# A second block product of the scan's gate in front of the attention scores, with buffers re-homed and the later order re-planned

## Chip, cores and metric

The kernel runs on one core of a Trainium2 chip. The metric is the device time of one execution in microseconds (us). "Before" is the kernel as it was, "after" the kernel with the change.

## What is computed

One decoder layer on 256 tokens of width 1024, batch 1, all in float32. Both branches, a gated linear recurrence (the "scan", HGRN2) and a softmax attention that here has one block of 256 keys, start from one normalised input and one wide projection:

```
h = rmsnorm(x, attn_norm_g)
hq, hf, hi, hg, aq, ak, av, gl = split(h @ w_in)
y_hg = (rmsnorm(scan(hq, hf, hi)) * silu(hg)) @ w_branch_hg
att  = softmax(rmsnorm(aq) . rmsnorm(ak) * scale + bias, causal) @ av
y_at = att @ w_branch_attn
merged = sigmoid(gl[0]) * y_hg + sigmoid(gl[1]) * y_at
x = x + merged @ w_out
x = x + (silu(n @ w_ffn_gate) * (n @ w_ffn_up)) @ w_ffn_down     with n = rmsnorm(x, ffn_norm_g)
```

There are 8 heads of width 128 in either branch.

## The kernel before

**Precision and halves.** Every float32 factor of a large product is split into a high half and a low half, both in the format fp32r. A weight block of 128 x 2048 numbers is loaded (`L:`), its high half is cast on ScalarE (ACT; step `h:`, line 500) and its low half, the difference, is made on VectorE (DVE; step `l:`, line 504). The matrix engine TensorE (PE) then makes the product (`M:`): for a block of 512 x 512 weights, eight 128x512 matmuls with the high half and then four with the low half (`product`, line 523). Three buffers each hold raw, high and low blocks in turn, so a new `h:` or `L:` also waits for the use of the third one before it.

**Seven products for eight.** The gates (`GS`, the silu gate of the scan; `GY` and `GZ`, the two sigmoid gates) are projected by a scheme with seven block products in place of eight. Products 1 and 2 take the weight blocks as they are (w11, w21). The others take sums that are made in place: block 5 is w11 + w12, block 6 adds w22 to that, block 7 is w12 + w22, block 4 is w21 plus the sum of block 6. Such a sum is either an addition on VectorE (`S:`, line 594) or a DMA that adds while it copies, issued from GpSimd's queue (`A:`, line 600); the tuple `BY_DMA` says which. So the sum of block 6 may be written only when both halves of block 5 are taken from the same buffer: `h:GS5`, `l:GS5`, `A:GS6`, `h:GS6`, `l:GS6`, `M:GS6` is a chain.

**The order.** The first part of the program, up to the attention scores, is ordered by the framework's scheduler by priority. From there on the order is written out by hand as two lists of names, `MIDDLE` and `FFN`; each name is one step, and each engine gets its steps in the order of the list. Every engine works strictly in its own order and waits where a step's input or a buffer is not ready. The stage of interest in `MIDDLE` has these steps:

- `scores` (PE line 482, DVE line 486): queries times keys; VectorE scales them and adds the bias, into `S0` (first 128 queries) and `S1` (last 128).
- `xa`, `xb0`, `xb1` (DVE 815): row maxima; `ea`, `eb0`, `eb1` (ACT 819): exponentials with their sums; `ma`, `mb0`, `mb1` (DVE 822, 823): division by the sums. `a` is `S0`, `b0` and `b1` are the two halves of the heads of `S1`.
- `M:p0` to `M:p5` (PE 839): transposes of the probabilities, through three PSUM banks in turn; `M:p0` and `M:p2` need `mb0`, `M:p1` and `M:p3` need `mb1`, the other two `ma`. `i:` copies each out on ScalarE (846, 851) and `k:` makes the low half on VectorE (853).
- `M:v` (PE 875, 878): probabilities times values, with the values' halves `vh` (ACT 863) and `vl` (DVE 866).
- `M:V2`, `M:V3` (PE 658): the projection of half of the values; `c:V0`, `c:V1` copy it out (ACT 905).
- `E3` to `E6`: levels of the scan (`k` ACT 379, `M` PE 394, `b` DVE 401, `q` DVE 416, `d` DVE 424).
- `Ch0`, `Ch1` (ACT 558) and `Cl0`, `Cl1` (DVE 561): halves of sums of the input that products 3, 5, 6 and 7 read.

In the kernel before only `GS1` stands in front of the scores; `GS2` stands in `MIDDLE`, between the transposes of the probabilities, because its weight block w21 is loaded into the buffer of the keys (home `T9`), which the scores read last.

**Homes.** Large buffers share named homes (`T1`, `T2`, ...): a buffer with the same tag may be written only when the last reader of the one before it is done.

Of the kernel before, what the change touches and what calls it, by code (L numbers as in the profile page):

```python
# [7 lines left out]
F32 = mybir.dt.float32  # L8
F32R = mybir.dt.float32r
# [18 lines left out]
def tile_hgrn2_moba_block(ctx: ExitStack, tc: tile.TileContext, xm, xw, table, runs,  # L28
# [3 lines left out]
    big = ctx.enter_context(tc.tile_pool(name="big", bufs=1))  # L32
# [123 lines left out]
    V0 = [pw(), pw()]  # L156
    V1 = [pw(), pw()]
# [10 lines left out]
    for kt in range(KT):  # L168
        i = kt % 2
# [4 lines left out]
        xk = packed[kt][:, 0:S] if kt else packed[kt][:, NV:NX]  # L174
# [30 lines left out]
    for q in range(2):  # L205
# [62 lines left out]
    R = big.tile([P, S], F32, name="R", tag="R")  # L268
# [74 lines left out]
    A = big.tile([P, 2, H, P], F32, name="A", tag="T5")  # L343
# [126 lines left out]
    def scores(qtok, qss, kT):  # L470
        rq = small.tile([P, 2, H], F32, name="rq")
        rinv(rq, qss, P)
        qT = head_T(qtok, "T10", "qT", qg[:, 0:1])
        S0 = big.tile([P, H, P], F32, name="S0", tag="T13")
        S1 = big.tile([P, H, S], F32, name="S1", tag="T7")
        for sc, tb, w, bt in ((S0, 0, P, B0), (S1, 1, S, B1)):
            m = 512 // w
            for g in range(H // m):
                bank = (pa, ph)[g % 2]()
                for i in range(m):  # L480
                    h = m * g + i
                    nc.tensor.matmul(bank[:, i * w:(i + 1) * w], qT[:, h, tb * P:(tb + 1) * P], kT[:, h, 0:w],
                                     start=True, stop=True)
                for i in range(m):
                    h = m * g + i
                    nc.vector.scalar_tensor_tensor(sc[:, h, :], bank[:, i * w:(i + 1) * w], rq[:, tb, h:h + 1],
                                                   bt[:, h, :], op0=OP.mult, op1=OP.add)
# [95 lines left out]
    def scheme(u, x, sums, bank_of, put):  # L583
# [14 lines left out]
        for k, a, other in (("5", "11", "12"), ("6", "11", "22"), ("7", "12", "22"), ("4", "21", "11")):  # L598
            if u.name + k in BY_DMA:
                todo[f"A:{u.name}{k}"] = lambda a=a, other=other: nc.gpsimd.dma_start(u.w[a], u.w[other], accum_op=OP.add)  # L600
# [21 lines left out]
            todo[("x:" if u.gate else "s:") + u.name + k] = lambda k=k, i=i, j=j: \  # L622
                put(i, j, banks[0] if k == "4" else q(i, j), j if k != "4" else 0)

    BY_DMA = ("GA4", "GA7", "GB4", "GB5", "GB7", "GS4", "GS5", "GS6", "GS7", "GY7", "GZ4", "GZ7", "UA4", "UA5", "UA7", "UB4", "UB7")

    four = []

# [13 lines left out]
    M = []  # L642
# [57 lines left out]
    hgrn_level(2)  # L700
    Va = big.tile([P, 2, D], F32, name="Va", tag="T1")
    put_tok(Va, tok_block(w_in, 6144, XT), 0)
    for name in ("L:V2", "L:V3", "L:GSw11", "h:GS1", "l:GS1", "M:GS1"):
        todo.pop(name)()
    S0, S1 = scores(qtok, qss, kT)
    hgrn_level(3, pa)

# [67 lines left out]
    oT = []  # L775
# [7 lines left out]

    def turned_o(g, m):
        if g % 2 == 0 and m == 0:
            oT.append(big.tile([P, 4, 2, S], F32R, name=f"oT{g // 2}", tag=("T6", "T9")[g // 2]))
        src = bank4(3).rearrange("p (h t) -> p h t", h=2)
        dst = [oT[g // 2][:, 2 * g % 4:2 * g % 4 + 2, k, :] for k in range(2)]
        if m == 0:
            nc.scalar.mul(dst[0], src, og)  # L790
        else:
            nc.vector.scalar_tensor_tensor(dst[1], src, og, dst[0].bitcast(F32), op0=OP.mult, op1=OP.subtract)
# [3 lines left out]
        todo[f"i:To{g}"] = lambda g=g: turned_o(g, 0)  # L796
        todo[f"k:To{g}"] = lambda g=g: turned_o(g, 1)

    GY = Unit("GY", w_in, 8192, ("T12", "T13"), ("T9", "T5", "T1", "T4"))
    GZ = Unit("GZ", w_in, 7168, "T4", ("T8", "T5", "T1", "T7"))  # L800

    for u in (GY, GZ):
        scheme(u, XT, sums, bank4, gate_of(u, AF.Sigmoid))
# [37 lines left out]
    def turned_p(n, m):  # L841
        hs, cs = slice(4 * (n % 2), 4 * (n % 2) + 4), turns_of[n][2]
        if cs is None:
            if n == 0:
                box["PT1"] = big.tile([P, H, P], F32, name="PT1", tag="T12")
            nc.scalar.copy(box["PT1"][:, hs, :], p_bank(n))
            return
        if ("P", m) not in box:
            box["P", m] = big.tile([P, H, S], F32R, name="P" + "hl"[m], tag=("T3", "T7")[m])
        if m == 0:  # L850
            nc.scalar.copy(box["P", 0][:, hs, cs], p_bank(n))
        else:
            nc.vector.tensor_sub(box["P", 1][:, hs, cs], p_bank(n), box["P", 0][:, hs, cs].bitcast(F32))
# [15 lines left out]
    aT = []  # L869
# [10 lines left out]

    def value_out(g, m):
        if not aT:
            aT.extend(big.tile([P, 4, 2, S], F32R, name=f"aT{i}", tag=("T7", "T3")[i]) for i in range(2))
        src = bank4(g).rearrange("p (h t) -> p h t", h=2)
        hi, lo = (aT[g // 2][:, 2 * g % 4:2 * g % 4 + 2, k, :] for k in range(2))
        if m == 0:
            nc.scalar.copy(hi, src)
        else:
            nc.vector.tensor_sub(lo, src, hi.bitcast(F32))
# [95 lines left out]
    r2 = small.tile([P, 2], F32, name="r2")  # L985
# [150 lines left out]
    def down(n, f0):  # L1136
# [40 lines left out]
        M:X s:GS4 f:GS2 c:X0 l:A0 s:GS2 M:O0 L:GYw22 c:X1 M:A0 e:O00 L:A3 l:A1 q:O00 h:GY1 f:GS3 L:H0 s:GS3 l:GY1
        M:O1 e:O01 S:GY5 q:O01 M:A1 L:GYw21 z:O01 A:GY7 h:GY5 e:O11 e:O10 q:O11 L:GZw11 l:GY5 q:O10 z:O11 M:GY1 r1
        h:A2 S:GY6 r2 l:A2 M:GY5 h:GY6 r3 L:H1 c:GY1 l:GY6 M:A2 n:O0 h:GY2 n:O1 l:GY2 M:GY6 L:GZw22 h:GY7 S:GY4
        c:GY5 M:To0 c:GY6 M:GY2 l:GY7 h:GY3 i:To0 l:GY3 L:GZw12 M:GY7 h:GY4 k:To0 l:GY4 M:GY3 h:A3 f:GY7 L:GZw21  # L1180
        l:A3 M:GY4 h:GZ1 s:GY7 l:GZ1 L:H2 M:To1 s:GY4 M:A3 i:To1 S:GZ5 k:To1 A:GZ7 h:GZ5 f:GY3 f:GY2 s:GY2 M:To2
        l:GZ5 M:GZ1 i:To2 h:H0 g:00 k:To2 s:GY3 M:GZ5 g:01 c:GZ1 l:H0 M:To3 c:GZ5 S:GZ6 M:H0 L:H3 i:To3 k:To3 h:GZ6
        g:11 g:10 h:GZ2 l:GZ6 M:GZ6 h:GZ7 l:GZ2 M:GZ2 c:GZ6 l:GZ7 A:GZ4 h:H1 M:GZ7 h:GZ3 l:H1 L:x2 f:GZ2 L:W0 M:H1
        h:H2 f:GZ7 l:GZ3 s:GZ2 s:GZ7 l:H2 mM:00 M:GZ3 L:W1 h:GZ4 aM:00 l:GZ4 M:m00 L:GBw11 h:H3 M:H2- f:GZ3 i:m00
        l:H3 M:GZ4 s:GZ3 k:m00 L:W2 M:H2+ s:GZ4 mM:01 aM:01 M:m01 h:W0 M:H3 i:m01 l:W0 h:W1 mM:10 L:W3 k:m01 aM:10
        M:W0- h:W2 mM:11 aM:11 l:W1 M:m11 M:m10 i:m11 M:W0+ i:m10 k:m10 L:a0 l:W2 h:W3 k:m11 M:W1 L:a1 l:W3 xa:00
# [113 lines left out]
```

## Time and profile before

| | us |
|---|---|
| median of 3 runs (lowest, highest) | 482.57 (481.52, 482.6) |
| the profiled execution, whole | 481.6 |
| its span, first to last instruction | 479.9 |
| TensorE busy within the span | 473.9 |
| VectorE, ScalarE, GpSimd busy | 409.1, 327.6, 48.1 |

The profiled execution lies 1.0 us under the median, and its span 1.7 us under its own time. TensorE is given as busy from a matmul's start to its modelled end, and back-to-back matmuls overlap, so the time of a product is best taken from the start of its first matmul to the start of the next product's. Starts are counted from the first instruction of the span.

### The profile page before, as it was taken

What the parts mean: (1) busy time and instruction counts of PE and PEld (TensorE: products, weight loads), DVE (VectorE), ACT (ScalarE), POOL (GpSimd) and SP (SyncE); (2) the same over time, 40 slices, a digit from 0 to 9 for tenths busy, and PEclk for the clock granted to TensorE, in tenths of its full rate; (3) what the DMA queues carried; (4) which work ended last, traced back from release to release, by engine and by line L of the source; (5) the groups of instructions that cost most, each with busy time, mean ns of one, the idle gap of its engine ahead of it and who ended that gap; (6) DMA issues with size and microseconds to landing.
All of it is one profiled execution on the core that took longest, in us unless ns stands there. A gap on an engine that the chain in (4) does not pass through costs nothing.

```text
span 479.9 us, 6451 instructions
## 1 busy us (share of the span) xinstructions
PE 473.9 (99%) x2502; PEld 397.6 (83%) x2502; DVE 409.1 (85%) x404; ACT 327.6 (68%) x439; POOL 48.1 (10%) x100
## 2 busy tenths in 40 slices
PE   9999999999999999999999999999999999999997
PEld 7888888888888788887888888888888888888886
DVE  6768999897669999879998787899999999887863
ACT  6978645768748998599767645776786558847520
POOL 1990220000000100000000000000000010010000
PEclk9999999999999999999999999999999999999999
DMA  8977595644359689895829856799979979996502
GB/s 305 402 259 259 155 332 177 205 144 157 111 149 246 132 210 384 272 275 180 255 92 263 271 201 229 260 273 230 355 240 219 342 188 266 374 262 145 176 0 87
DMA packets 44557, 108.97 MB, mean 227 GB/s; under 512 B 1896, under 2 KB 4200, under 8 KB 42352
## 3 DMA queue, kind: packets, MB, share of 16 engines
q1 hardware_dynamic: 41344, 88.11, 53.0%
q0 software_dynamic: 3184, 20.47, 20.2%
q8 instruction: 19, 0.31, 0.3%
q14 instruction: 10, 0.08, 0.0%
HBM read 89.67 MB, written 1.07 MB: 189 GB/s over the span
## 4 chain that ended last, share of the span: by engine, by line
PE 97%; ACT 1%; DVE 1%; issue 0%; DVEq 0%
PE pw L658 14%; PE acc L1145 12%; PE late L523 12%; PE f L523 8%; PE pw L101 6%; PE pw L165 5%; PE pw L1040 5%; PE pa L523 3%; PE pw L83 3%; PE pw L84 3%; PE pw L85 3%; PE pw L523 3%; PE f L658 2%; PE pw L100 2%; PE pw L103 2%; PE pw L1039 1%
## 5 line engine op out<-in xcount | busy, mean ns | idle before, releaser
L504 DVE TENSOR_TENSOR wlo<-W,whi 128x2048 fp32r<-128x2048 f32 x44 | 100.2, 2288 | 14.3 <-ACT whi L500 14.2
L500 ACT CAST whi<-W 128x2048 fp32r<-128x2048 f32 x44 | 83.7, 1913 | 41.9 <-DVE W L594 22.8
L504 DVE TENSOR_TENSOR wlo<-wraw,whi 128x2048 fp32r<-128x2048 f32 x36 | 82.2, 2287 | 12.2 <-ACT whi L500 12.1
L500 ACT CAST whi<-wraw 128x2048 fp32r<-128x2048 f32 x36 | 68.9, 1914 | 11.9 <-PE pw L658 5.3
L56 DVE TENSOR_TENSOR wlo<-wraw,whi 128x2048 fp32r<-128x2048 f32 (+1 forms) x20 | 41.5, 2079 | 8.9 <-ACT whi L55 8.8
L101 PE MATMUL pw<-XT,whi 128*128 128x512 f32 x128 | 40.6, 395 | 0.0
L55 ACT CAST whi<-wraw 128x2048 fp32r<-128x2048 f32 (+1 forms) x20 | 34.6, 1736 | 7.4 <-PE pw L101 4.7
L600 POOL DMA_DIRECT2D W<-W x13 | 11.1, 853 | 238.6 <-DVE W L594 96.5
L1040 PE MATMUL pw<-x2T,whi 128*128 128x512 f32 x96 | 31.3, 397 | 0.0
L1145 PE MATMUL acc<-whi,hq 128*128 128x512 f32 x92 | 29.3, 393 | 0.0
L594 DVE TENSOR_TENSOR W<-W,W 128x2048 f32<-128x2048 f32 x11 | 25.2, 2288 | 0.3
L83 PE MATMUL pw<-whi,XT 128*128 128x512 f32 x64 | 25.2, 394 | 0.0
L85 PE MATMUL pw<-whi,XT 128*128 128x512 f32 x64 | 25.0, 391 | 0.0
L84 PE MATMUL pw<-wlo,XT 128*128 128x512 f32 x64 | 24.9, 390 | 0.0
L523 PE MATMUL late<-whi,C 128*128 128x512 f32 x96 | 23.8, 390 | 0.0
L523 PEld LDWEIGHTS late<-whi,C 128*128 128x128 f32 x96 | 18.0, 188 | 3.7
L658 PE MATMUL pw<-whi,oT 128*128 128x512 f32 x64 | 20.7, 394 | 0.0
L658 PE MATMUL pw<-whi,aT 128*128 128x512 f32 x64 | 20.6, 393 | 0.0
L658 PE MATMUL pw<-whi,M 128*128 128x512 f32 x64 | 20.4, 394 | 0.0
L1145 PEld LDWEIGHTS acc<-whi,hq 128*128 128x128 f32 x92 | 17.3, 188 | 3.5
L101 PEld LDWEIGHTS pw<-XT,whi 128*128 128x128 f32 x128 | 19.8, 189 | 0.2
L523 PE MATMUL late<-whi,x2T 128*128 128x512 f32 x72 | 18.1, 394 | 0.0
(349 smaller groups left out, 1135.2 us busy)
## 6 DMA issues: line engine op xcount, KB each, us to landing
wraw<-w_in SPq DMA_DIRECT2D x21, 1024.0 KB, 5.2
W<-W POOLq DMA_DIRECT2D x13, 1024.0 KB, 9.4
wraw<-w_down SPq DMA_DIRECT2D x11, 1024.0 KB, 8.7
W<-w_in SPq DMA_DIRECT2D x9, 1024.0 KB, 7.4
W<-w_gate SPq DMA_DIRECT2D x8, 1024.0 KB, 7.3
W<-w_up SPq DMA_DIRECT2D x8, 1024.0 KB, 7.7
wraw<-w_at SPq DMA_DIRECT2D x4, 1024.0 KB, 7.3
wraw<-w_hg SPq DMA_DIRECT2D x4, 1024.0 KB, 6.3
```

The source lines that it names most:

```text
L55: high = nc.scalar.copy(hi, src)
L56: return high, nc.vector.tensor_sub(lo, src, hi.bitcast(F32))
L83: nc.tensor.matmul(ps[tb], part(act, kt, 0)[:, ts], wh, start=(kt == 0), stop=False)
L84: nc.tensor.matmul(ps[tb], part(act, kt, 0)[:, ts], wl, start=False, stop=False)
L85: nc.tensor.matmul(ps[tb], part(act, kt, 1)[:, ts], wh, start=False, stop=(kt == KT - 1))
L101: nc.tensor.matmul(ps[ct], hi[:, i, cs], both, start=(kt == 0), stop=(kt == KT - 1))
L500: nc.scalar.copy(t["hi"], raw())
L504: nc.vector.tensor_sub(t["lo"], raw(), t["hi"].bitcast(F32))
L523: nc.tensor.matmul(bank, act(kt, m), h[:, kt, :], start=(first and n == 0), stop=(n == 11), skip_group_check=True)
L658: nc.tensor.matmul(blocks[key][tb], part(act, k0 + i, m)[:, tb * P:(tb + 1) * P], t[w][:, i, :], start=(k0 + i == 0 and m == 0 and w == "hi"),
L1040: nc.tensor.matmul(block["ps", up][ct], t["hi"][:, i, cs], both, start=(kt == 0), stop=(kt == KT - 1))
L1145: nc.tensor.matmul(bank, ACTS[f0 + i](m, ts), w[:, i, c0:c0 + cw], start=(st and i == 0 and m == 0 and w is t["hi"]), stop=(en and i == 1 ...
```

## The change

1. `GS2` goes in front of the scores, behind `GS1`. Its weight block is loaded early, into home `T7`, which the keys by token (`ktok`) leave after they are transposed.
2. Homes are dealt anew: the gate's result `GS` moves from `T8` to `T9` (the keys' home, free after the scores), the scores `S1`, the low half of the probabilities and the first part of the attention's result `aT0` move from `T7` to `T8`, and buffers of later stages that share these homes move with them.
3. The first weight sum of the second sigmoid gate, `GZ5`, is made by an adding DMA in place of an addition on VectorE.
4. The list `MIDDLE` is planned anew. No matmul is added or left out, and the list `FFN` is as it was.

```
-        S1 = big.tile([P, H, S], F32, name="S1", tag="T7")
+        S1 = big.tile([P, H, S], F32, name="S1", tag="T8")
...
-    BY_DMA = (... "GY7", "GZ4", "GZ7", ...)
+    BY_DMA = (... "GY7", "GZ4", "GZ5", "GZ7", ...)
...
-    GS = Unit("GS", w_in, 3072, "T8", (None, "T9", None, None))
+    GS = Unit("GS", w_in, 3072, "T9", (None, "T7", None, None))
...
-    for name in ("L:V2", "L:V3", "L:GSw11", "h:GS1", "l:GS1", "M:GS1"):
+    for name in ("L:GSw21", "L:V2", "L:V3", "L:GSw11", "h:GS1", "l:GS1", "M:GS1", "h:GS2", "l:GS2", "M:GS2"):
         todo.pop(name)()
...
-            oT.append(big.tile([P, 4, 2, S], F32R, name=f"oT{g // 2}", tag=("T6", "T9")[g // 2]))
+            oT.append(big.tile([P, 4, 2, S], F32R, name=f"oT{g // 2}", tag=("T6", "T7")[g // 2]))
...
-    GY = Unit("GY", w_in, 8192, ("T12", "T13"), ("T9", "T5", "T1", "T4"))
-    GZ = Unit("GZ", w_in, 7168, "T4", ("T8", "T5", "T1", "T7"))
+    GY = Unit("GY", w_in, 8192, ("T12", "T13"), ("T7", "T5", "T1", "T4"))
+    GZ = Unit("GZ", w_in, 7168, "T4", ("T9", "T5", "T1", "T8"))
...
-            box["P", m] = big.tile([P, H, S], F32R, name="P" + "hl"[m], tag=("T3", "T7")[m])
+            box["P", m] = big.tile([P, H, S], F32R, name="P" + "hl"[m], tag=("T3", "T8")[m])
...
     MIDDLE = """
-        ma eb0 l:GS5 M:E4 c:V0 mb0 A:GS6 c:V1 M:GS5 eb1 b:E4 q:E4 k:E5 M:p0 mb1 M:p2 i:p0 M:E5 h:GS2 Cl1 M:p1 M:p3
+        Cl1 ma eb0 l:GS5 M:E4 eb1 M:GS5 mb0 A:GS6 c:V0 q:E4 c:V1 M:p0 vh mb1 i:p0 k:E5 b:E4 M:p1 M:p2 n:E4 i:p1 M:p3
```

The three places that matter here follow as the instructions stand. First TensorE between the last product of the values' first half and the transposes of the queries (line 457); `XT` is the input, whose second half GS2 reads, and `pw` a PSUM bank.

```order
 L523 MATMUL pw<-whi,XT_73 128x512 x8
 L523 MATMUL pw<-wlo,XT_73 128x512 x4
+L523 MATMUL pw<-whi,XT_74 128x512 x8
+L523 MATMUL pw<-wlo,XT_74 128x512 x4
 L457 MATMUL pa<-ident,qtok 128x128 x4
 L457 MATMUL ph<-ident,qtok 128x128 x4
```

GS2's twelve matmuls stand in front of the queries' transposes, and so of the scores and of all that comes from them.

Next TensorE behind GS5, between its twelve matmuls and those of GS6; `f_` are the PSUM banks, `S_1370` and `S_1371` are `S0` and `S1` before. Before it stands so:

```order
L839 MATMUL f_1458<-ident,S_1371 128x128 x4
L839 MATMUL f_1460<-ident,S_1371 128x128 x4
L394 MATMUL f_1461<-QA,KP 64x2x32 x16
L839 MATMUL f_1459<-ident,S_1371 128x128 x4
L839 MATMUL f_1458<-ident,S_1371 128x128 x4
L839 MATMUL f_1459<-ident,S_1370 128x128 x4
L523 MATMUL pw<-whi,XT_74 128x512 x8
L523 MATMUL pw<-wlo,XT_74 128x512 x4
L839 MATMUL f_1460<-ident,S_1370 128x128 x4
L523 MATMUL pw<-whi,C 128x512 x8
L523 MATMUL pw<-wlo,C 128x512 x4
```

And in the changed kernel, where `S_1389` and `S_1390` are `S0` and `S1`:

```order
L839 MATMUL f_1475<-ident,S_1390 128x128 x4
L839 MATMUL f_1476<-ident,S_1390 128x128 x4
L839 MATMUL f_1477<-ident,S_1390 128x128 x4
L839 MATMUL f_1475<-ident,S_1390 128x128 x4
L839 MATMUL f_1476<-ident,S_1389 128x128 x4
L394 MATMUL f_1478<-QA,KP 64x2x32 x16
L839 MATMUL f_1477<-ident,S_1389 128x128 x4
L523 MATMUL pw<-whi,C 128x512 x8
L523 MATMUL pw<-wlo,C 128x512 x4
```

GS2 is gone from between the transposes, `p1` stands directly behind `p0`, and from GS5 to GS6 only the six transposes and one scan level are left.

Last ScalarE from the copies of the values to the high half of GS6; `PT` and `Ph` are the copies of the transposed probabilities, and the last row holds `h:GS6` and `h:GS7`. After:

```order
L905 ACTIVATE Va<-f_1475,rx 128x512
L905 ACTIVATE Va<-f_1477,rx 128x512
L863 CAST Vh<-Va 128x1024
L846 COPY PT_1614<-f_1475 128x512
L379 COPY KP<-K 128x2x16x32
L846 COPY PT_1614<-f_1476 128x512
L851 CAST Ph<-f_1477 128x4x128
L851 CAST Ph<-f_1476 128x4x128
L851 CAST Ph<-f_1475 128x4x128
L618 COPY q<-pw 128x512
L851 CAST Ph<-f_1477 128x4x128
L500 CAST whi<-wraw 128x2048 x2
```

Before, `h:GS6` is the cast in the fourth row of this piece, ahead of the copy of `p5`:

```order
L846 COPY PT_1600<-f_1459 128x512
L851 CAST Ph<-f_1458 128x4x128
L851 CAST Ph<-f_1459 128x4x128
L500 CAST whi<-wraw 128x2048
L618 COPY q<-pw 128x512
L863 CAST Vh<-Va 128x1024
L851 CAST Ph<-f_1460 128x4x128
L500 CAST whi<-wraw 128x2048
```

In the changed kernel `h:GS6` stands behind the copies of all six transposes.

More of the change, by code (lines that the diff above doesn't have):

```diff
@@ L623, in scheme @@
                 put(i, j, banks[0] if k == "4" else q(i, j), j if k != "4" else 0)
-    BY_DMA = ("GA4", "GA7", "GB4", "GB5", "GB7", "GS4", "GS5", "GS6", "GS7", "GY7", "GZ4", "GZ7", "UA4", "UA5", "UA7", "UB4", "UB7")
+    BY_DMA = ("GA4", "GA7", "GB4", "GB5", "GB7", "GS4", "GS5", "GS6", "GS7", "GY7", "GZ4", "GZ5", "GZ7", "UA4", "UA5", "UA7", "UB4", "UB7")
     four = []
@@ L882, in value_out @@
         if not aT:
-            aT.extend(big.tile([P, 4, 2, S], F32R, name=f"aT{i}", tag=("T7", "T3")[i]) for i in range(2))
+            aT.extend(big.tile([P, 4, 2, S], F32R, name=f"aT{i}", tag=("T8", "T3")[i]) for i in range(2))
         src = bank4(g).rearrange("p (h t) -> p h t", h=2)
@@ L923, in mixed @@
         if M[half] is None:
-            M[half] = big.tile([P, 4, 2, S], F32R, name=f"M{half}", tag=("T8", "T9")[half])
+            M[half] = big.tile([P, 4, 2, S], F32R, name=f"M{half}", tag=("T9", "T8")[half])
         hi, lo = (M[half][:, :, k, tb * P:(tb + 1) * P] for k in range(2))
@@ L1171, in tile_hgrn2_moba_block @@
     MIDDLE = """
-        h:V2 l:V2 L:GSw12 h:V3 l:V3 L:GSw22 L:GSw21 A:GS5 M:V2 Ch0 k:E4 xa Ch1 xb0 ea xb1 M:V3 Cl0 d:E4 A:GS7 h:GS5
-        ma eb0 l:GS5 M:E4 c:V0 mb0 A:GS6 c:V1 M:GS5 eb1 b:E4 q:E4 k:E5 M:p0 mb1 M:p2 i:p0 M:E5 h:GS2 Cl1 M:p1 M:p3
-        b:E5 i:p2 l:GS2 i:p1 i:p3 M:p4 M:GS2 i:p4 h:GS6 k:p2 A:GS4 k:p4 k:p3 c:GS1 M:p5 l:GS6 vh M:GS6 i:p5 h:GS7
-        k:p5 vl c:GS6 n:E4 M:v c:GS5 l:GS7 h:GS3 L:A0 d:E5 L:A1 h:GS4 l:GS3 k:E6 M:GS7 L:GYw12 i:v3 q:E5 L:A2 i:v2
-        i:v1 k:v3 sp k:v1 M:GS3 i:v0 f:GS7 h:A0 l:GS4 M:E6 h:A1 n:E5 L:GYw11 k:v2 M:GS4 q:E6 s:GS7 d:E6 k:v0 b:E6
@@ L1177, in tile_hgrn2_moba_block @@
[L1177 to L1186, printed above, removed]
@@ L1187, in tile_hgrn2_moba_block @@
-        xj:t00 M:t00 xa:01 h:a0 M:W2- xg:t00 xi:t00 M:t01 l:a0 M:W2+ xj:t01 xg:t01 xk:t00 xi:t01 xk:t01 M:W3 h:a1
-        l:a1 xa:10 xj:t10 M:t10 xa:11 M:a0- xg:t10 xj:t11 xi:t10 R:s M:t11 R:a M:a0+ R:q xg:t11 xk:t10 xi:t11 R:r
-        R:n xk:t11 M:a1 L:GBw12 L:b0
+        h:V2 l:V2 L:GSw12 h:V3 l:V3 L:GSw22 A:GS5 M:V2 Ch0 k:E4 xa c:GS1 Ch1 xb0 ea xb1 M:V3 Cl0 d:E4 A:GS7 h:GS5
+        Cl1 ma eb0 l:GS5 M:E4 eb1 M:GS5 mb0 A:GS6 c:V0 q:E4 c:V1 M:p0 vh mb1 i:p0 k:E5 b:E4 M:p1 M:p2 n:E4 i:p1 M:p3
@@ new lines, in tile_hgrn2_moba_block @@
+        d:E5 i:p2 M:p4 M:E5 k:p2 i:p4 i:p3 k:p4 M:p5 c:GS5 k:p3 A:GS4 i:p5 vl h:GS6 k:p5 b:E5 h:GS7 l:GS6 M:GS6 k:E6
+        l:GS7 sp M:v c:GS6 q:E5 L:A0 h:GS4 L:A1 n:E5 d:E6 h:GS3 l:GS4 M:GS7 L:GYw12 i:v3 i:v2 L:GYw11 k:v3 i:v0 k:v2
+        i:v1 k:v0 M:E6 h:A0 f:GS7 k:v1 M:GS4 q:E6 s:GS7 b:E6 l:GS3 M:X s:GS4 c:X0 h:A1 M:O0 l:A0 L:GYw22 L:A2 c:X1
+        M:GS3 f:GS2 L:A3 l:A1 s:GS2 M:A0 h:GY1 e:O00 L:H0 f:GS3 q:O00 l:GY1 s:GS3 S:GY5 M:O1 e:O01 A:GY7 h:GY5 e:O10
+        q:O01 l:GY5 M:A1 L:GYw21 q:O10 e:O11 z:O01 L:GZw11 S:GY6 q:O11 z:O11 M:GY1 h:A2 r1 r2 l:A2 M:GY5 h:GY6 r3
@@ new lines, in tile_hgrn2_moba_block @@
+        L:H1 n:O0 l:GY6 M:A2 h:GY2 c:GY1 l:GY2 n:O1 M:GY6 L:GZw22 h:GY7 S:GY4 c:GY5 l:GY7 M:To0 c:GY6 M:GY2 i:To0
+        h:GY3 k:To0 L:GZw12 M:GY7 l:GY3 h:GY4 l:GY4 M:To1 h:A3 M:GY3 f:GY7 i:To1 L:GZw21 l:A3 s:GY7 M:GY4 h:GZ1
+        f:GY2 L:H2 l:GZ1 s:GY2 M:A3 s:GY4 h:GZ2 g:01 A:GZ5 k:To1 l:GZ2 g:00 M:GZ1 h:H0 f:GY3 g:11 s:GY3 l:H0 M:To2
+        c:GZ1 M:GZ2 i:To2 A:GZ7 h:GZ5 k:To2 L:H3 g:10 M:To3 l:GZ5 h:H1 M:H0 i:To3 l:H1 k:To3 L:W0 S:GZ6 M:GZ5 f:GZ2
+        A:GZ4 h:GZ6 M:H1 h:GZ3 l:GZ6 c:GZ5 l:GZ3 s:GZ2 mM:00 M:GZ6 h:GZ7 aM:00 l:GZ7 M:GZ3 c:GZ6 h:H2 L:x2 l:H2
@@ new lines, in tile_hgrn2_moba_block @@
+        M:GZ7 h:GZ4 f:GZ3 L:W1 M:m00 L:GBw11 s:GZ3 f:GZ7 M:H2- h:H3 l:GZ4 M:GZ4 i:m00 l:H3 s:GZ7 M:H2+ s:GZ4 k:m00
+        L:W2 mM:01 aM:01 M:m01 h:W0 M:H3 i:m01 l:W0 h:W1 k:m01 L:W3 mM:10 aM:10 M:W0- h:W2 mM:11 aM:11 l:W1 M:m10
+        M:m11 i:m10 M:W0+ i:m11 k:m10 L:a0 k:m11 l:W2 M:W1 h:W3 L:a1 l:W3 xa:00 xj:t00 M:t00 xa:01 h:a0 M:W2- xg:t00
+        xi:t00 M:t01 l:a0 M:W2+ xj:t01 xg:t01 xk:t00 xi:t01 xk:t01 M:W3 h:a1 l:a1 xa:10 xj:t10 M:t10 xa:11 M:a0-
+        xg:t10 xj:t11 xi:t10 R:s M:t11 R:a M:a0+ R:q xg:t11 xk:t10 xi:t11 R:r R:n xk:t11 M:a1 L:GBw12 L:b0
```

## The prediction

> **What bounds the kernel now.** I read the page first, then who waited for whom on TensorE.
>
> ```profile
> span 479.9 us, 6451 instructions
> PE 473.9 (99%) x2502; PEld 397.6 (83%) x2502; DVE 409.1 (85%) x404; ACT 327.6 (68%) x439; POOL 48.1 (10%) x100
> ```
>
> ```profile
> PE f L839 <- ACT PT L846: 0.9, 1, 0.9
> PE f L523 <- DVE q L621: 0.5, 1, 0.5
> PE f L875 <- DVE Vl L866: 0.3, 1, 0.3
> ```
>
> TensorE is the bound from end to end. No matmul is added or removed, so the change can move the time only by TensorE's waits. Behind the start-up there are three: for a copy of transposed probabilities, for an addition of the gate GY and for the low half of the values. The timeline of TensorE shows two of them.
>
> ```profile
> 134.63 1.98 PE L523 MATMUL pw<-whi,XT 128*128 128x512 f32 x8
> ...
> 137.35 0.60 PE L457 MATMUL pa<-ident,qtok 128*128 128x128 f32 x4
> ...
> 144.56 1.15 PE L394 MATMUL pa<-QA,KP 128*64 128x64 f32 x32
> ...
> 157.84 2.11 PE L523 MATMUL pw<-whi,C 128*128 128x512 f32 x8
> ...
> 160.69 1.03 PE L839 MATMUL f<-ident,S 128*128 128x128 f32 x8
> 161.66 1.15 PE L394 MATMUL f<-QA,KP 128*64 128x64 f32 x32
> ...
> 164.74 0.66 PE L839 MATMUL f<-ident,S 128*128 128x128 f32 x4 [0.91 <-ACT PT L846]
> ...
> 168.01 0.60 PE L839 MATMUL f<-ident,S 128*128 128x128 f32 x4
> 168.37 2.11 PE L523 MATMUL pw<-whi,C 128*128 128x512 f32 x8
> 170.32 1.09 PE L523 MATMUL pw<-wlo,C 128*128 128x512 f32 x4
> 171.25 0.28 PE L875 MATMUL f<-Ph,Vh 128*128 128x256 f32 x1
> ...
> 176.37 2.09 PE L523 MATMUL pw<-whi,C 128*128 128x512 f32 x8
> ```
>
> From the top: GS1 (start 134.63, so 2.72 a product until 137.35), the queries' transposes, the end of the scores (144.56), GS5 (157.84), p0 and p2 (160.69), E5, p4 after the wait (164.74), p5, GS6 (168.37, its low half from 170.32), the values (171.25), GS7 (176.37). How full the other engines are in this stretch, in the busy time by windows (columns: length, PE, PEld, DVE, ACT, POOL, clock, DMA share, GB/s):
>
> ```profile
> 145.60:176.40 30.80, 29.59 (x217) 24.91 (x213) 30.40 (x35) 29.89 (x56) 2.57 (x3) 1.00 0.77 170
> ```
>
> Behind the scores VectorE (30.40 of 30.80) and ScalarE (29.89) are as full as TensorE: three engines in balance. In front of the scores they are not, as the idle times in brackets show (two timelines, VectorE and ScalarE):
>
> ```profile
> 137.35 2.29 DVE L504 TENSOR_TENSOR wlo<-wraw,whi 128x2048 fp32r<-128x2048 f32 x1 [3.55 <-ACT whi L500]
> ...
> 144.67 0.88 DVE L486 SCALAR_TENSOR_TENSOR S<-ph,rq,B 128x256 f32<-128x256 f32 x2
> 145.76 0.78 DVE L401 COPY_PREDICATED A<-mask,pa 128x256 f32<-128x256 uint32 x2 [0.21 <-PE pa L394]
> ...
> 157.39 0.17 DVE L822 RECIPROCAL smb<-smb 128x4 f32<-128x4 f32 x1
> ...
> 158.74 0.78 DVE L401 COPY_PREDICATED A<-mask,f 128x256 f32<-128x256 uint32 x2
> 159.40 1.22 DVE L416 TENSOR_TENSOR QA<-QA,F 128x1024 f32<-128x1024 f32 x1
> ...
> 161.89 1.22 DVE L561 TENSOR_TENSOR C<-C 128x1024 fp32r<-128x1024 f32 x1
> 163.02 0.77 DVE L401 COPY_PREDICATED A<-mask,f 128x256 f32<-128x256 uint32 x2
> ```
>
> ```profile
> 145.58 1.05 ACT L558 CAST C<-C 128x1024 fp32r<-128x1024 f32 x1 [5.17 <-DVE S L486]
> ...
> 152.95 1.90 ACT L500 CAST whi<-wraw 128x2048 fp32r<-128x2048 f32 x1
> ...
> 161.33 0.58 ACT L846 COPY PT<-f 128x512 f32<-128x512 f32 x1 [0.45 <-PE f L839]
> ...
> 164.09 0.60 ACT L846 COPY PT<-f 128x512 f32<-128x512 f32 x1
> 164.57 0.61 ACT L851 CAST Ph<-f 128x512 fp32r<-128x512 f32 x1
> ...
> 165.92 1.92 ACT L500 CAST whi<-wraw 128x2048 fp32r<-128x2048 f32 x1
> ```
>
> **GS2 in front.** Its halves (1.9 on ScalarE, 2.29 on VectorE) go into idle time, so both are done before GS1 ends. The price: the transposes and scores come one product later, 2.72. The scores feed the softmax, and both full engines start their queue behind the scores' last row: VectorE at 145.76 + 2.72 = 148.48, ScalarE at 148.30 (its first step waited for that row, 5.17). Each is relieved of about 2 us and started 2.7 us later; TensorE keeps the same work up to GS6 and loses its filler between the transposes. The early load of w21 costs nothing: it waits for the keys' transposes, whose last start at
>
> ```profile
> L457 PE MATMUL ph<-ident,ktok x8: 272/272/273, 109.7 to 111.9; 128*128 128x128 f32 x8
> ```
>
> some 20 us ahead of GS1's end, and its later load in the busy stretch goes.
>
> **The queue of VectorE.** From 145.76 to 157.39 (11.63) stand all steps through `l:GS5`; now `Cl1` (163.02 - 161.89 = 1.13) stands among them too. So `l:GS5` ends at 148.48 + 11.63 + 1.13 = 161.24. `mb0`, E4's two steps and `mb1` took 161.89 - 157.39 = 4.50; E4's copy (159.40 - 158.74 = 0.66) now comes behind `mb1`, which ends at 161.24 + 4.50 - 0.66 = 165.08. ScalarE is no later: `h:GS5` ended 9.3 behind its first step, and with the copy of GS1 now among them (0.5) it ends at 158.05, before VectorE comes to it at 159.0.
>
> **TensorE behind GS5.** Up to GS5 nothing waits, so p0 starts at 160.69 + 2.72 = 163.41. p1 stands right behind it and needs `mb1`: it starts at 165.2, a wait of 1.3. Before, p1 had GS2's place and E5 ahead of it.
>
> **ScalarE up to GS6.** A copy starts 0.64 behind its transpose (160.69, 161.33) and takes 0.48 (164.09 to 164.57). p1's copy runs 165.84 to 166.32; p4 takes p1's bank, so it starts at 166.5, E5 at 167.0, p5 at 168.05, whose copy ends at 169.2. Only then stands `h:GS6` (1.92): 171.1. The other condition for it is the sum of block 6, a DMA that may start once `l:GS5` is done:
>
> ```profile
> 157.77 0.85 POOL L600 DMA_DIRECT2D wraw<-wraw  x1 [4.61 <-DVE smb L822]
> ```
>
> ```profile
> DMA to landing us min/median/max: 6.9/6.9/6.9
> ```
>
> It left about 0.3 behind the end of `l:GS5` and took 6.9 (the landing of this one DMA): now 161.6 + 6.9 = 168.5, so 0.7 of slack. GS6 starts at 171.1, where TensorE was free from 168.5: a wait of 2.6. `l:GS6` (2.29, behind a step of E5 on VectorE) ends near 173.55; the low half would start 1.95 behind the high one, at 173.05, so 0.5 more. The four low matmuls take 0.93 (171.25 - 170.32): the values start at 174.5. They took 176.37 - 171.25 = 5.12 with a wait in them (0.31 idle, about 0.45 from start to start) that goes, since `vl` now comes early. GS7 starts at 179.2, against 176.37: **+2.8**.
>
> **What comes back later.** Steps behind this have more room, since TensorE is later and the two others are not. The third wait:
>
> ```profile
> 225.36 1.07 PE L523 MATMUL f<-wlo,C 128*128 128x512 f32 x4
> 226.94 2.08 PE L523 MATMUL f<-whi,XT 128*128 128x512 f32 x8 [0.51 <-DVE q L621]
> ```
>
> Without it the second row would start at 226.28; it goes, **-0.7**, since a transpose now stands in front of GY3 and VectorE is ahead. GZ5's sum by DMA frees VectorE by one addition (2.3, as the eleven additions of line 594, 2288 ns each on the page); TensorE waits for nothing there, so I take 0. If that DMA took the longest time below, 12.3, it would still have the products GZ1, GZ2 and H0 as cover (48 matmuls of 2.72 / 12 = 0.227, 10.9) with two transposes beside them; beyond that each us costs one. The homes cost 0 too: each new tenant comes behind a reader that stood about as far ahead as before.
>
> Sum: 2.8 - 0.7 = +2.1. On the profiled execution: span 482.0, time 481.6 + 2.1 = 483.7. Against the median, which lies 1.0 higher, **484.7**. Bounds: were `h:GS6` half a us earlier and the wait of the low half gone, 483.7; were the late wait to stay and the landing or the copies 0.5 later, 485.9. With the spread of the runs, this case alone reaches from 483.3 to 486.
>
> [...] The start of the program shows that TensorE runs slower at first: the same three matmuls
>
> ```profile
> 4.84 1.65 PE L165 MATMUL pw<-whi,XT 128*128 128x512 f32 x3
> ...
> 6.96 0.86 PE L165 MATMUL pw<-whi,XT 128*128 128x512 f32 x3
> ```
>
> take 1.65 and then 0.86, while the clock's column stays at 1.00. After the wait of 0.91 at 164.74 nothing was slow. The waits that I forecast are 1.3 and 2.6. If the longer one brings the slow rate back for as long as at the start (some 5.8 us), half of that is lost, 2.9: 487.6. [...]
>
> **Rivals.**
> - *The idle time pays.* The halves of GS2, now made in idle time, let the transposes come without waits, and all three old waits go: about 1.1 (0.91 idle, seen from start to start), 0.45 and 0.67, in all 2.2, so 480.4. For it: the idle 3.55 and 5.17. Against: the queues behind the scores start 2.72 later for it. It decides at p1: `mb1` would have to end by 163.9, and `h:GS6` by 167.5. Chance 0.10.
> - *The sum of block 6 lands late.* It shares GpSimd's queue with the sum of block 7. The sum of block 5 took, before,
>
> ```profile
> DMA to landing us min/median/max: 12.3/12.3/12.3
> ```
>
>   with two loads beside it. Halfway, at 9.6, it would land at 171.2, 2.0 behind ScalarE: 486.7. Against: the loads that ran beside it are over by then. Chance 0.10.
> - *The slow rate returns* (above): 487.6, chance 0.05, since nothing slow follows the one wait seen.
>
> **Numbers.** The forecast has 0.75. A measurement of this kernel can tell about 0.3% (1.45 us) from no change: the part of the forecast under 484.0 counts as that, 0.20 by its bounds, the rest, 0.55, as slower. With the rivals: slower 0.55 + 0.10 + 0.05 = 0.70, same 0.20, faster 0.10. The range holds the forecast with the spread of the runs and the second rival's midpoint: 482.6 to 486.8; the first rival, the last and the late half of the second, near 0.2, lie outside.
>
> **What would show it.** Right: a wait of some 1.3 of TensorE for VectorE's line 823 in front of the second transpose; one of 2 to 3 in front of GS6 for ScalarE's line 500; GS7 starting near 179; no wait near 229; the same spacing of matmuls after the waits. Wrong: transposes without a wait, or `h:GS6` released by the DMA instead of by its place behind the copies (the second rival), or a new wait behind 180, where I count none.

## The result, and the profile after

The change makes the kernel slower: 483.7 us in the median of 10 runs (483.39 to 484.47), against 481.54 of the kernel before on the same chip (10 runs, 480.69 to 482.6). The ratio is 1.0051, its 95% interval 1.0043 to 1.0059. The profiled execution took 483.51 us.

First two lines of the page of the changed kernel, and the whole answer on who waits for whom on TensorE (us in total, times, longest):

```profile
span 481.8 us, 6463 instructions
...
PE 473.4 (98%) x2502; PEld 397.1 (82%) x2502; DVE 407.7 (85%) x403; ACT 327.7 (68%) x439; POOL 52.3 (11%) x101
```

```profile
PE pw L523 <- ACT whi L500: 2.5, 1, 2.5
PE f L839 <- DVE S L823: 1.3, 1, 1.3
PE warm L153 <- DVE ones L148: 1.1, 1, 1.1
PE pw L523 <- DVE wlo L504: 0.3, 1, 0.3
```

TensorE is as busy as it was (473.4 for 473.9). The three old waits behind the start-up are gone, and three new ones have come: for a half of the softmax (L823), for the high half of GS6 (L500) and for its low half (L504). The timeline of TensorE of the changed kernel shows where they lie:

```profile
134.10 1.98 PE L523 MATMUL pw<-whi,XT 128*128 128x512 f32 x8
...
136.82 1.98 PE L523 MATMUL pw<-whi,XT 128*128 128x512 f32 x8
...
162.88 0.60 PE L839 MATMUL f<-ident,S 128*128 128x128 f32 x4
164.79 1.96 PE L839 MATMUL f<-ident,S 128*128 128x128 f32 x16 [1.31 <-DVE S L823]
166.68 1.15 PE L394 MATMUL f<-QA,KP 128*64 128x64 f32 x32
167.76 0.66 PE L839 MATMUL f<-ident,S 128*128 128x128 f32 x4
170.89 2.12 PE L523 MATMUL pw<-whi,C 128*128 128x512 f32 x8 [2.47 <-ACT whi L500]
173.34 1.20 PE L523 MATMUL pw<-wlo,C 128*128 128x512 f32 x4 [0.34 <-DVE wlo L504]
...
178.89 2.09 PE L523 MATMUL pw<-whi,C 128*128 128x512 f32 x8
```

From the top: GS1, GS2, p0, then p1 to p4 behind the first wait, E5, p5, GS6 behind the second, its low half behind the third, and GS7. What was late is on the other engines, in the timelines of the changed kernel: VectorE's step `mb1`; on ScalarE the first step behind the scores, the copy of p5 and `h:GS6` (in one row with `h:GS7`); and on GpSimd the DMA that adds up block 6.

```profile
163.42 1.23 DVE L823 TENSOR_TENSOR S<-S,smb 128x1024 f32<-128x1024 f32 x1
```

```profile
147.77 1.05 ACT L558 CAST C<-C 128x1024 fp32r<-128x1024 f32 x1 [5.17 <-DVE S L486]
...
168.45 0.59 ACT L851 CAST Ph<-f 128x512 fp32r<-128x512 f32 x1
168.94 3.71 ACT L500 CAST whi<-wraw 128x2048 fp32r<-128x2048 f32 x2
```

```profile
161.10 0.85 POOL L600 DMA_DIRECT2D wraw<-wraw  x1 [7.09 <-DVE smb L822]
```

`mb1` ends at 164.65 and p1 starts right behind. The DMA was issued at 161.10 and took 6.9 from issue to landing, so it landed at 168.0, 0.9 ahead of `h:GS6`. `h:GS6` starts as soon as the copy of p5 in front of it is done, with no idle time in brackets: nothing but its place on ScalarE held it. ScalarE's queue behind the scores starts at 147.77, where 148.30 was forecast.

Losses are counted in what follows from one matmul's start to the next, less the usual spacing of that kind, to about 0.1. Behind the start-up, before: 1.07 + 0.47 + 0.67 = 2.21. After: 1.47 + 2.63 + 0.50 = 4.60. The difference is 2.4; 0.5 of it is hidden in the two spans, because the execution of before had lost 0.5 more at its start (GS1 at 134.63 there, at 134.10 here, with the same work in front of it). So the spans differ by 1.9.

### The profile page after: what moved, and what is told of

Same layout as the page of the kernel before. It is cut to its first block, busy times and chain, and to the rows that moved or that the text cites. A ratio compares the mean times of both kernels' runs of the same rounds, so it can differ in the third digit from the quotient of the medians.

```text
span 481.8 us, 6463 instructions
## 1 busy us (share of the span) xinstructions
PE 473.4 (98%) x2502; PEld 397.1 (82%) x2502; DVE 407.7 (85%) x403; ACT 327.7 (68%) x439; POOL 52.3 (11%) x101
## 3 DMA queue, kind: packets, MB, share of 16 engines
HBM read 89.67 MB, written 1.07 MB: 188 GB/s over the span
## 4 chain that ended last, share of the span: by engine, by line
PE 94%; DVE 4%; issue 1%; ACT 0%
PE pw L658 14%; PE acc L1145 12%; PE late L523 12%; PE f L523 8%; PE pw L101 6%; PE pw L1040 5%; PE pw L165 5%; PE pa L523 3%; PE pw L523 3%; PE pw L83 3%; PE pw L85 3%; PE pw L84 3%; PE pw L103 2%; PE pw L100 2%; PE pw L1039 1%; PE pw L1042 1%
## 5 line engine op out<-in xcount | busy, mean ns | idle before, releaser
L500 ACT CAST whi<-W 128x2048 fp32r<-128x2048 f32 x44 | 83.7, 1914 | 43.9 <-DVE W L594 20.5
L504 DVE TENSOR_TENSOR wlo<-W,whi 128x2048 fp32r<-128x2048 f32 x44 | 100.1, 2288 | 15.7 <-ACT whi L500 15.5
L504 DVE TENSOR_TENSOR wlo<-wraw,whi 128x2048 fp32r<-128x2048 f32 x36 | 81.9, 2287 | 14.0 <-ACT whi L500 14.0
L500 ACT CAST whi<-wraw 128x2048 fp32r<-128x2048 f32 x36 | 68.6, 1912 | 14.2 <-PE pw L658 8.2
L594 DVE TENSOR_TENSOR W<-W,W 128x2048 f32<-128x2048 f32 x10 | 22.9, 2288 | 0.3
```

Of the source, the lines that this page charges most:

```text
L500: nc.scalar.copy(t["hi"], raw())
L504: nc.vector.tensor_sub(t["lo"], raw(), t["hi"].bitcast(F32))
```

## The experiments

**The theory** is that of the prediction: GS2 in front of the scores puts the scores, and the full queues of VectorE and ScalarE behind them, one product later, and takes TensorE's filler from between the transposes. The rivals: the sum of block 6 lands late; the homes or the adding DMA cost; the new order costs.

### The parts one by one

`homes_only` is the kernel before with the new homes and with GZ5's sum by DMA:

```
+    tags of S1, GS, oT1, GY, GZ, Pl, aT0, M as in the changed kernel
+    "GZ5" in BY_DMA, and A:GZ5 for S:GZ5 in the old MIDDLE
```

> All of the change but GS2's move: the new homes and GZ5's sum by DMA, with GS2 in its old place and the old order. Queue theory (the loss comes from GS2's move alone: the scores and the two full queues behind them start one product later, and no product is left to cover the transposes): as before, ratio to before 1.000, within 0.001; the wait near p4 (0.9) stands. Rival (the homes or the added DMA cost): 1.002 or more, with a wait of TensorE behind 180 for a load or for line 500.

Measured: 487.53 us, ratio 1.0129 (1.0116 to 1.0142). A miss by 6 us, and the waits of TensorE say where:

```profile
PE f L523 <- ACT whi L500: 3.1, 1, 3.1
PE pw L658 <- DVE wlo L504: 1.4, 1, 1.4
```

GpSimd, ScalarE and TensorE around the first, in this kernel:

```profile
230.75 0.85 POOL L600 DMA_DIRECT2D W<-W  x1 [31.07 <-DVE wlo L504]
```

```profile
239.49 1.90 ACT L500 CAST whi<-W 128x2048 fp32r<-128x2048 f32 x1 [8.98 <-DMA W<-W]
```

```profile
241.44 3.45 PE L523 MATMUL f<-whi,C 128*128 128x512 f32 x8 [3.12 <-ACT whi L500]
244.72 1.08 PE L523 MATMUL f<-wlo,C 128*128 128x512 f32 x4
```

The adding DMA is issued at 230.75, the cast that needs it starts 8.7 later, and in the old order not enough work stands between. In the changed kernel the same DMA is issued at 234.77 and lands 8.2 later, at 243.0; the product that needs it, GZ5, starts at 249.48. And the eight matmuls behind the wait take 3.45 in place of 1.98. The windows of this kernel say why (the clock is the third number from the end):

```profile
240.00:240.90 0.90, 0.00 (x0) 0.00 (x0) 0.00 (x0) 0.90 (x1) 0.78 (x1) 1.00 0.00 0
240.95:244.36 3.41, 2.92 (x7) 2.34 (x8) 2.94 (x3) 3.41 (x5) 0.00 (x0) 0.50 0.95 192
244.40:246.00 1.60, 1.60 (x11) 1.30 (x10) 1.60 (x3) 1.23 (x3) 0.00 (x0) 1.00 1.20 246
```

The granted clock was halved from 240.95, 2.6 into the wait, for 3.41 us. The two idle times, 3.12 and 1.35, and the 1.5 that the eight matmuls took longer make 5.9 of the 6 us in this execution. One of the four runs shows a mean clock of 1.0 and took no less, 487.57; no trace shows where it lost the rest.

`front_only` also has GS2 in front, and the old order with only GS2's four steps taken out:

```
-    L:GSw21 ... h:GS2 ... l:GS2 ... M:GS2      (out of the old MIDDLE, into the front)
```

> GS2 in front with the new homes, but the old order with GS2's steps taken out. Queue theory: the scores are late here too and the filler is gone too; p1 has E5 in front of it again, so it waits little, but h:GS6 comes behind four copies and the copy of GS1 behind that, so GS6 starts near 170, and the values wait for their low half: 1.5 to 2.2 us over before, ratio 1.003 to 1.0045. Rival (the new order is at fault, not the move): as before or faster, 1.000 or less.

Measured: 490.98 us, ratio 1.0196 (1.0181 to 1.0211), a miss for the same reason: the DMA of GZ5 lost what it lost in `homes_only`. In the stage itself TensorE lost 0.64 at the transposes, 2.69 at GS6 and 0.46 at the values, 3.8 in all where before lost 1.54.

So both were run again with the sum left on VectorE (`"GZ5"` out of `BY_DMA`, `S:GZ5` at its old place). `homes_dve5`:

> The kernel before with the new homes alone: GZ5's sum stays on VectorE, GS2 stays among the transposes, the order is the old one. Theory (homes are free; the 6.0 us that homes and the adding DMA together lost in the old order are all the DMA's): 1.000 times before, within 0.001, and the three old waits of TensorE (0.9, 0.5, 0.3) with nothing beside them. Rival (the homes themselves cost or pay, since a new tenant waits for another reader): a ratio of 1.002 or more, or 0.998 or less, with a wait that names one of the re-homed buffers.

Measured: 481.07 us, ratio 0.9997 (0.9988 to 1.0005), the three old waits and no other. The homes cost nothing; all 6 us were the DMA's.

`front_dve5`, the move alone:

> GS2 in front of the scores with the new homes, GZ5's sum on VectorE, and the old order with only GS2's steps taken out: the move by itself. Theory (the move shifts scores and the full queues by a product and takes the filler): the waits of the earlier run with the adding DMA, 0.64 among the transposes, 2.69 in front of GS6, 0.46 in front of its low half, and 0.67 at the late addition, 4.5 in all against 2.2 before: 2.2 us slower, 1.0047 times before, about what the whole change costs, so that the new order gains next to nothing in this stage. Rival (the move is sound and the new order is what costs): 1.000 or less.

Measured: 484.66 us, ratio 1.0059 (1.0046 to 1.0071). Two of the five runs, the profiled one among them, show a mean clock of 1.0 and took 483.45 and 483.46, 2.2 over the kernel before; the other three, at 0.996, took 1.2 to 1.4 more. The waits of the profiled run:

```profile
PE pw L523 <- ACT q L618: 2.5, 1, 2.5
...
PE f L839 <- ACT PT L846: 0.5, 1, 0.5
PE f L523 <- DVE q L621: 0.5, 1, 0.5
PE f L875 <- DVE Vl L866: 0.3, 1, 0.3
```

From start to start they are 2.69, 0.67, 0.67 and 0.46, in all 4.49. GS6 waits here for the copy of GS1's result (line 618), which stands on ScalarE behind `h:GS6`. The move by itself costs what the whole change costs; the rival that blames the new order falls.

`after_dve5` is the changed kernel with GZ5's sum back on VectorE, at the same place of the new order:

> The changed kernel with GZ5's sum back on VectorE, at the same place of the order. Theory (in the new order the adding DMA lies under the products GZ1, GZ2 and H0, and TensorE waits for VectorE nowhere there, so the DMA pays nothing and costs nothing): the time of the changed kernel, 1.005 times before, within 0.001. Rival (the DMA or its neighbours cost time that the waits don't show): 1.003 or less; or VectorE needs the relief: 1.007 or more, with a wait of TensorE between 225 and 250.

Measured: 485.47 us, ratio 1.0082 (1.0070 to 1.0094), with one wait more, on TensorE's timeline and on VectorE's:

```profile
245.25 0.66 PE L781 MATMUL f<-ident,o 128*128 128x128 f32 x4 [1.12 <-DVE oT L792]
```

```profile
242.25 2.28 DVE L504 TENSOR_TENSOR wlo<-wraw,whi 128x2048 fp32r<-128x2048 f32 x1
244.46 0.74 DVE L792 SCALAR_TENSOR_TENSOR oT<-f,vec,oT 128x512 fp32r<-128x512 f32 x1
```

That is 1.29 from start to start, for a step of To2 (a transpose of the scan's output) that stands on VectorE behind the addition and all it pushed back. VectorE does need the relief: expected was no difference to the changed kernel, so a miss, and the rival that names the relief came. In the old order the adding DMA loses 6 us, in the new one it gains about 1.3.

### What decides inside the stage

`no_sum6` is the changed kernel without the DMA that adds up block 6; that sum is left out, the rest is as it was.

```
-    A:GS6
```

> The changed kernel without the adding DMA of block 6 (GS6 then reads the sum of block 5; that part of the computation is left out). Queue theory: h:GS6 is held by its place on ScalarE behind the copy of p5, so nothing changes: as after within 0.2 us, ratio to before 1.005. Rival (the landing of that DMA decides): GS6 starts earlier by what the landing was late, 1 us or more, ratio 1.003 or less.

Measured: 483.82 us, ratio 1.0057 (1.0045 to 1.0069), and the same waits to the tenth:

```profile
PE pw L523 <- ACT whi L500: 2.5, 1, 2.5
PE f L839 <- DVE S L823: 1.3, 1, 1.3
```

The landing of that DMA decides nothing, as expected; this rival falls.

`gs2_behind` keeps GS2's load and halves in front and puts its twelve matmuls behind the scores:

```
-    for name in (... "h:GS2", "l:GS2", "M:GS2"):
+    for name in (... "h:GS2", "l:GS2"):
...
-        h:V2 l:V2 ...
+        M:GS2 h:V2 l:V2 ...
```

> The changed kernel with GS2's halves still made in front of the scores, but its product listed behind them (three of its twelve matmuls come to stand among the scores' matmuls, nine behind). Queue theory: the softmax starts about 2 us earlier, p1 no longer waits; GS6 still waits for its high half behind the copies, about 2, since nothing covers it: 0.6 to 1.1 us under after, ratio to before 1.003. Rival A (only the late scores count): 3 us or more under after, ratio 0.999 or less. Rival B (only the missing filler counts): as after, 1.005.

Measured: 484.64 us, ratio 1.0074 (1.0062 to 1.0087); the one of its six runs with a mean clock of 1.0, the profiled one, took 483.52, the others, at 0.996 or 0.993, 0.9 to 2.4 more. TensorE in the profiled run:

```profile
163.38 1.93 PE L839 MATMUL f<-ident,S 128*128 128x128 f32 x16
166.09 0.66 PE L839 MATMUL f<-ident,S 128*128 128x128 f32 x4 [0.78 <-ACT PT L846]
...
170.89 2.11 PE L523 MATMUL pw<-whi,C 128*128 128x512 f32 x8 [2.47 <-ACT whi L500]
```

`mb1` is 1.3 earlier and the wait at p1 is gone, but GS6 starts at 170.89 as in the changed kernel. On ScalarE the copy of the keys for E5 (1.05) stands between the copies of p0 and p1, so p4 waits for its bank, and `h:GS6` stands behind the copy of p5 as before. Counted from GS1's start (134.38 here, 134.10 there) GS6 comes only 0.3 earlier than in the changed kernel, where 0.6 to 1.1 was expected: a miss, nearer to rival B. To bring the scores forward is not enough. That the order of ScalarE's copies takes the gain back is read from the trace; no run puts `h:GS6` ahead of the copies in the changed kernel.

### Can the idle time be made to pay?

If TensorE idles in front of GS6 because nothing that is ready stands there, a part of the values' product (24 matmuls of line 875, 2.8 us) can be put there. `v_split` does that in the changed kernel:

```
+    todo["M:w"] = values_late        # the matmuls of line 878
...
-    i:p5 vl h:GS6 k:p5 b:E5 ... M:GS6 ... M:v
+    i:p5 vl k:p5 M:v h:GS6 b:E5 ... M:GS6 ... M:w
```

> The changed kernel with the product of probabilities and values cut in two: its part with the halves (24 matmuls, 2.8 us) stands in front of GS6, the rest behind it, and the copies that follow are put in that order. Theory (TensorE stands idle in front of GS6 only because nothing that is ready stands there, while ScalarE comes to the high half late): the wait of 2.5 in front of GS6 shrinks to a wait of 1.2 to 1.6 for the values' low half, GS7 starts at 177.3 in place of 178.9, and the kernel is 1.4 to 1.7 us under the changed one, 1.002 times before. Rival (the time is set by ScalarE's and VectorE's queues behind GS6, so the filler only moves the wait to GS7 or behind): GS7 within 0.4 of 178.9 and 1.004 or more.

`replanned` adds to it GS2's product behind the scores and `k:E5` in front of the transposes:

> GS2's halves in front of the scores, its product directly behind them; the values' product cut in two as in the run beside it; the copy of the keys for the scan's level E5 in front of the transposes. Theory (idle time of the two others pays once the scores are not put off and a filler stands in each gap): of TensorE's waits only one of about 1.2 for the values' low half is left behind the scores, 1 us or so less than before in all, 0.997 to 0.999 times before. Rival (VectorE and ScalarE are full behind the scores, so the idle time can't pay): 1.001 or more.

In these two, level E5's copy reads its bank behind the values' product, and GS7's addition reads its bank behind GS4's product, so that a part of the scan and of the gate is not the reference's. Measured: `v_split` 484.81 us, ratio 1.0072 (1.0058 to 1.0086), and `replanned` 483.51 us, ratio 1.0044 (1.0032 to 1.0057); both miss, and the rivals' figures came. The wait of 2.5 in front of GS6 is gone in both, but two others came, here in `replanned`:

```profile
PE pw L523 <- DVE wlo L504: 1.2, 1, 1.2
...
PE f L737 <- ACT A L721: 0.9, 1, 0.9
PE f L875 <- DVE Vl L866: 0.6, 1, 0.6
PE f L875 <- DVE Pl L853: 0.3, 1, 0.3
```

The first came of my order: VectorE's copy for E5 waited 2.37 for the values' product in front of it, and GS6's low half behind that copy. So `v_split2` and `replanned2` have `b:E5` (in `replanned2` with `d:E5` behind it) ahead of `M:v`, the addition of GS7 ahead of GS4, and ScalarE's tail in the order `c:X0 h:A0 ... c:X1 h:A1`; they compute the whole reference.

> The changed kernel, its GS2 in front as it is, with the values' product cut in two: the part with the halves (24 matmuls, 2.8 us) stands in front of GS6, behind the copy of level E5, the rest behind GS6, and the steps up to the scan's output in that order. All of the reference is computed. Theory (TensorE idles in front of GS6 because nothing that is ready stands there): the wait of 1.3 at the second transpose stays, one of about 1.2 for the values' halves comes, those of 2.5 and 0.3 go, GS7 starts near 177.3 and nothing waits behind it: losses of 2.7 in place of 4.6, about 1.9 us under the changed kernel, 1.001 times before. Rival (VectorE's and ScalarE's full queues only hand the wait on to GS7 or to the scan): 1.004 or more.

> GS2's halves in front of the scores, its product directly behind them, the values' product cut in two as in the run beside it, level E5's copy of the keys in front of the transposes and its update of the keys behind the values' halves. All of the reference is computed. Theory (the idle time in front of the scores pays once the scores are not put off and each gap has a filler): no wait over 0.4 of TensorE behind the scores, losses of 0.5 or less in place of 2.2 before, 1.7 us faster, 0.996 to 0.998 times before. Rival (the two other engines are full behind the scores and hand the wait on): 1.001 or more.

Measured: 486.08 us, ratio 1.0091 (1.0077 to 1.0106), and 485.38 us, ratio 1.0074 (1.0061 to 1.0087): two more misses, with the rivals' figures again. The one run of each with a mean clock of 1.0 took 484.00 and 483.89, the others 1.2 to 2.7 more. Up to GS7 `v_split2` went as expected; `replanned2` had waits of 0.3 and 0.6 at the values, where none over 0.4 was expected, and GS7 started at 176.66. Then, in `replanned2` (TensorE, VectorE, and a window):

```profile
183.25 2.53 PE L523 MATMUL pw<-whi,XT 128*128 128x512 f32 x8 [2.50 <-DVE q L621]
185.59 1.91 PE L523 MATMUL pw<-wlo,XT 128*128 128x512 f32 x4
```

```profile
179.63 2.28 DVE L504 TENSOR_TENSOR wlo<-W,whi 128x2048 fp32r<-128x2048 f32 x1
181.83 0.68 DVE L891 TENSOR_TENSOR aT<-f,aT 128x512 fp32r<-128x512 f32 x1
182.43 0.68 DVE L621 TENSOR_TENSOR q<-q,pw 128x512 f32<-128x512 f32 x1
```

```profile
185.00:186.00 1.00, 1.00 (x3) 0.72 (x3) 0.97 (x2) 0.00 (x0) 0.00 (x0) 0.50 0.97 356
```

The addition of GS7 (line 621) stood on VectorE behind the low half of GS4 and a copy, GS4 waited 2.5 for it, and the clock was halved once more. `replanned3` moves it, and the copies of the values on ScalarE, ahead, and `d:E5` back among the transposes:

```
-    l:GS7 sp M:w c:GS6 h:GS4 q:E5 ... i:v3 k:v3 ... M:GS7 ... i:v0 i:v1 i:v2 l:GS4 ... k:v0 M:E6 h:GS3 f:GS7
+    l:GS7 sp M:w c:GS6 q:E5 ... i:v3 i:v0 k:v3 n:E5 d:E6 h:GS4 ... k:v0 i:v1 i:v2 M:GS7 ... f:GS7 l:GS4 ... M:E6
```

> The plan before it (GS2's halves in front of the scores, its product behind them, the values' product in two parts), with the addition for GS7 on VectorE put in front of the low half of GS4 and of two copies of the values, and the copies of the values on ScalarE put in front of GS4's high half. All of the reference is computed. Theory (it was the place in VectorE's full queue that made GS4 wait 2.5): that wait goes, the two in front of the values (0.3 and 0.6 of idle time, 1.3 from start to start) stay, and up to 0.5 comes at the scan's output: losses of 1.3 to 1.8 in place of 2.2 before, and no stretch at half clock: 0.998 to 0.999 times before. Rival (VectorE has no room left behind the scores, so the wait moves on once more): a wait of 1 or more behind GS4, 1.001 or more.

Measured: 481.16 us in the median of 12 runs, ratio 0.9997 (0.9988 to 1.0006). Its waits:

```profile
PE late L523 <- ACT q L618: 0.7, 1, 0.7
PE f L875 <- DVE Vl L866: 0.6, 1, 0.6
PE f L875 <- DVE Pl L853: 0.3, 1, 0.3
PE late L523 <- DVE wlo L504: 0.2, 1, 0.2
```

In the stage and up to the end of the second gate the losses at waits are 0.49 + 0.80 + 0.23 = 1.5, as expected, 0.7 less than before, and the gain of 0.5 to 1 us that should follow is not there. The trace shows that the count leaves something out: from GS1's start to the start of the feed-forward part's first product (line 523) it took 179.60, against 179.72 before, so 0.1 was gained and not 0.7, as the medians say too. A part is seen where three of GS2's matmuls stand among those of the scores: from GS1 to the scan level behind the scores it took 10.83, 0.68 of it for the three, against 9.93, so 0.2 was lost without a wait. The profiled execution, at 483.94 us the longest of the 12, lost 2.1 more than before in the feed-forward part, whose order was not touched (the lines `late` above are the idle part of it), and 0.35 at its start; the other eleven took 480.79 to 481.48.

## Why the prediction was right

**The sign and the size.** Forecast was a loss of 2.1 on the profiled execution, and the medians on one chip differ by 483.7 - 481.54 = 2.2. The forecast of 484.7 is 1.0 too high because the median of three runs given at first, 482.57, lay 1.0 above that of ten. That 2.1 and 2.2 lie so close is in part luck: on the two profiled executions the stretch from GS1's start to the feed-forward part's first product grew by 2.45 (182.17 for 179.72).

**p1.** Forecast: a wait of 1.3 for `mb1`. Measured: 1.31 idle, 1.47 from start to start. p0 and p1 were put at 163.41 and 165.2 and came at 162.88 and 164.79: the 0.5 of the start-up and no more.

**GS6.** Forecast: `h:GS6` done at 171.1 behind the six copies, a wait of 2.6, another 0.5 for the low half. Measured: start at 170.89, 2.47 idle (2.63 from start to start), then 0.34 idle (0.50). Counted from GS1's start GS6 came 0.3 later than forecast (36.79 for 36.47), which is what the sum for GS7 is short. That the DMA is no part of it is shown by `no_sum6`; the place on ScalarE is read from the trace, where `h:GS6` follows the copy of p5 without idle time. That place is not the whole of it either: in `front_dve5` `h:GS6` stands ahead of the last copy, and GS6 waits as long for the next step of the same queue. The other reason, the scores one product later, is not enough by itself: `gs2_behind` takes 1.3 of that lateness away and GS6 moves by 0.3, since by the trace the order of ScalarE's copies takes the rest back.

**GS7 and the late wait.** GS7 was put at 179.2 and came at 178.89. From GS1's start it came 44.79 later in place of 41.74, so +3.05 where the sum had +2.8. The wait near 229 is gone as forecast, and `front_dve5` shows that it is the new order that takes it away: with the old one it stays (0.67).

**Terms of nothing.** The homes: shown (`homes_dve5`). GZ5's DMA: it cost nothing, but the reason beside it, that TensorE waits for nothing there, was read from the old order. In the new one VectorE's addition would cost 1.3 (`after_dve5`), and in the old one the DMA would have cost 6 (`homes_only`). The cover that the prediction named (GZ1, GZ2, H0) is the new order's, and without it the term would have been wrong.

**The rivals.** That the idle time pays did not come: it needed the product behind the scores, the values' product cut in two and a new order of both queues, and then it pays back what the move cost and no more (`replanned3`, 2.5 us under the changed kernel, no faster than before). The sum of block 6 is out (`no_sum6`). The slow clock did not come in the profiled execution, where the clock stayed at 1.0, but was nearer than the 0.05 given: one of the ten runs, the longest at 484.47, shows a mean clock of 0.996, as those experiments did in which it was seen halved for 3.4 us, and `gs2_behind`, with waits of the same size, does so in five of six.

## What to carry to other kernels

Where three engines are full, read a move by the place that its work leaves: the matmuls that stood between two waits were cover, and taking them to a stage with idle time cost as much as two new waits while the idle time gained nothing. An adding DMA in place of an addition here gained 1.3 us or cost 6, by the products that stand between its issue and its first reader, so a DMA and the order that covers it are one edit and are costed together. A wait mended in an order by hand comes up again at the next step behind the same queue until that step has been moved too: follow each full queue to the first place where it has slack before a gain is booked.

## What the runs showed of the hardware

The granted clock is the surprise. With a wait of 3.12 it was halved for 3.41 us (`homes_only`), and with one of 2.50 too, for about 3.4 (`replanned2`), where eight matmuls took 2.53 and the four behind them 1.91 in place of 1.07; yet with the wait of 2.47 in the profiled execution of the changed kernel it stayed at 1.00. The halving did not begin at the same point in the two: at 240.95 in `homes_only`, 0.5 before the matmuls begin again, and in `replanned2` at about 184.68, 1.4 after they have begun, to end at about 188.1 (worked out from the mean clocks of 0.84 and 0.95 in the windows from 184 to 185 and from 188 to 189). What sets its start, and why the wait of 2.50 came with it and that of 2.47 did not, no run here shows.
